# A two-layer trunk on one core: 1/rms from one full product and a power of 256 columns, caches and memory handed in as they are used

## The chip, the cores and the metric

The kernel runs on one core of a Trainium2 chip. Its engines take their instructions in the order in which they are written: TensorE (PE; PEld is its weight load), VectorE (DVE), ScalarE (ACT), GpSimd (POOL), and SyncE (SP), which here only issues transfers; ACT and POOL issue some as well. The metric is the device time of one execution in microseconds, from the start of the program to its end, with inputs and weights in the chip's memory.

## What is computed

Two layers; 128 prompt tokens and 128 sample tokens go through the same weights, so that all products run on 256 columns, one for each token. A layer is a half-step of a gated FFN, a token mixer (differential attention, a 2-D Fourier transform and a bidirectional mLSTM, merged with gates) and a second half-step. Ahead of each of the three stands a norm with modulation:

```python
def rms_norm(x, g):
    y = xf * lax.rsqrt(jnp.mean(xf * xf, axis=-1, keepdims=True) + EPS)
    return (y * g).astype(x.dtype)

u  = modulate(rms_norm(x, g[1]), sh2, sc2)      # x * (1 + scale) + shift
z  = u @ w_in
# sample tokens: keys and values are [cached | own], own keys rotated
k_use = concatenate([k_ctx, apply_rope(k, cos, sin)]); v_use = concatenate([v_ctx, v])
# mLSTM of the sample tokens starts from the cached memory C0, n0, m0
x = x + gt2 * token_mixer(u)
```

The prompt tokens' keys, values and final memories are outputs (`new_cache_k`, `new_cache_v`, `new_state_C` and two small ones), beside the two token blocks.

## The kernel before, in words

**Layout.** The state `xT` is [128, 8, 256]: feature within a block of 128, block k = 0..7, token. A weight comes in chunks of 1 MB (`raw`, by SP), and each chunk is split into a high part `whi` (a cast on ACT, L1523) and a low part `wlo` (a subtraction on DVE, L1524); so is each activation (`hilo`, L177 and L178). Every product with a weight is three matmuls (`mm3`, L165 to L168): high by high, high by low, low by high. Small products and transposes in plain float32 go through `mm` (L163) and `trans` (L171). `pm`, `pa`, `pb` are tiles of PSUM.

**Order.** The order is the order of the code. A list of `steps` (units of the projections) is run from first to last; small work of the attention, Fourier, gate and mLSTM parts is written as generators, "lanes", each `yield` of which ends one lane step. A lane step is run from the middle of a product of eight blocks (`mid`), so that a lane's matmuls stand between those of the projections in TensorE's row. The splits of coming weight chunks are pumped in the same manner.

**A norm.** While the residual is added block by block, `square` squares the block on ACT and POOL adds it into `nsum` [128, 256] (L413; the last square stays apart as `last`), and `block`/`parts` make y = x * (1 + scale), not yet divided by the rms, with its high and low part (`yf` L426, `yh` L177, `yl` L178). The last two blocks are held back (`held`). Then `first` (L523) starts the next projection: four units (512 columns of the weight) on y, for k = 0 to 7. After k = 0 it makes 1/rms: `stats` sums over the features with four matmuls of one column each (`pb` 128x2), `root` makes `var` on DVE (L463) and the power -1/2 on POOL (L465), `diag` puts the two columns of 1/rms on the diagonals of two matrices `dg` (one on DVE, L469, one on ACT), and `spread`, after k = 1, multiplies a matrix of ones with them, so that all partitions hold the row of 256 values, which ACT copies from PSUM to `bcs`. Then `apply` makes u = y * bcs + shift in two halves of four blocks: L486 (times), L491 (plus), `uh` on ACT (L492), `ul` on DVE (L495). The four units on y are corrected with `bcs` as they leave PSUM (`scaled`, L552). All further products of the projection read u. `first` is called five times: for the two mixers and for three FFNs; the first norm of the program and the last one are made in another way.

**Caches and memory.** In a mixer, `loads` and `loads2` issue the transfers of the narrow gate weights `zgw` (on POOL) and of the cached keys and values `ckv` and the memory `C0` (on ACT), each rearranged by the transfer's access pattern. The attention lane transposes the four heads' cached keys (L171 into `pa`) and copies them into the first half of `kl`, has the rotary swap of q brought into the other half of `kl` by four transfers (L822), rotates, does the same for k, transposes the prompt's k for the output `new_cache_k` (copy `kctx` on ACT, transfer on POOL), and comes to scores, softmax and values (transposed probabilities `pc`). The gate lane transposes the eight blocks of `C0` into `c0t`.

Of the kernel before, what the change touches and what calls it, by code (L numbers as in the profile page):

```python
# [14 lines left out]
ALU = mybir.AluOpType  # L15
AX = mybir.AxisListType

P = 128
D = 1024
# [3 lines left out]
H = 4  # L23
# [99 lines left out]
def trunk_kernel(ctx: ExitStack, tc: tile.TileContext, a: dict):  # L123
# [12 lines left out]
    def blk(shape, name, dt=F32):  # L136
        return blkp.tile(shape, dt, tag="blk", name=name)
# [4 lines left out]
    def t2(shape, name, dt=F32):  # L142
        return tp.tile(shape, dt, tag="t2", name=name, bufs=N_T2)
# [240 lines left out]
    class Norm:  # L384
# [81 lines left out]

        def diag(self):
            dg = self.dg = t2([P, 2, P], "dg")
            ve.tensor_scalar(dg[:, 0, :], ident, self.rstd[:, 0:1], None, op0=ALU.mult)  # L469
            ac.activation(dg[:, 1, :], ident, AF.Copy, scale=self.rstd[:, 1:2])  # L470

        def spread(self):
            bc = pb([P, 256])
            mm(bc, ones, flat(self.dg))
            self.bc = tmp([P, 256], "bcs", bufs=1)
            ac.copy(self.bc, bc)

        def apply(self):
# [44 lines left out]
    def first(norm, us, done, func=None):  # L523

        ps = first_tiles()
        for k in range(KD):
            first_k(norm.yk, k, us, ps)
            if k == 0:
                norm.stats()
                warm(func)  # L530
                held.pop(0)()
                norm.diag()
                while held:
                    held.pop(0)()
                pump_split(1)
            if k == 1:
                norm.spread()
        norm.apply()
        pump_split(1)

        def rest():
            done(norm, ps)
            pump_split()

        late.append(rest)
# [146 lines left out]
    def add_mixer(l, norm, norm_next, mods_):  # L692
# [3 lines left out]
        def loads():  # L696
            M["zgw"] = tmp([P, KD, 16], "zgw", bufs=1)
            po.dma_start(out=M["zgw"], in_=w_in[:, 4096:4112].rearrange("(k p) f -> p k f", p=P))

        def loads2():  # L700
            ac.preload_act_table_set("natural_log_exp_and_others")
            M["ck"] = blk([P, 2, H, P], "ckv")
            nc.scalar.dma_start(out=M["ck"][:, 0], in_=a["cache_k"][0, l].rearrange("h s d -> s h d"))
            nc.scalar.dma_start(out=M["ck"][:, 1], in_=a["cache_v"][0, l].rearrange("h s d -> s h d"))
            M["C0"] = blk([P, 2, H, P], "C0")
            nc.scalar.dma_start(out=M["C0"], in_=a["state_C"][0, l].rearrange("d h v k -> v d h k"))
            gh, gl = M["gh"], M["gl"] = blk([P, KD, 104], "zgh", F32R), blk([P, KD, 104], "zgl", F32R)
# [95 lines left out]
        def attn_lane():  # L803
            q = M["q"]
            ql = q[:, :, T:]
            kl = blk([P, H, 256], "kl")
            yield
            yield
            t = pa([P, H, P])
            for h in range(H):  # L810
                trans(t[:, h, :], M["ck"][:, 0, h, :])
            yield
            ve.tensor_copy(kl[:, :, 0:128], t)
            cosb = cst[:, C_COS:C_COS + 128].unsqueeze(1).to_broadcast([P, H, T])
# [21 lines left out]
            yield  # L836
            t = pa([P, H, P])
            for h in range(H):
                trans(t[:, h, :], k[:, h, 0:T])
            yield  # L840
            kn = t2([P, H, P], "kctx")
            ac.copy(kn, t)
            po.dma_start(out=a["new_cache_k"][0, l].rearrange("h s d -> s h d"), in_=kn)
            yield
# [115 lines left out]
            for h in range(H):  # L960
                for c in range(2):
                    vv = M["ck"][:, 1, h, :] if c == 0 else M["v"][:, 1, h * P:(h + 1) * P]
                    mm(o[:, h, :], pTl[h // 2][:, 2 * (h % 2) + c, :], vv, start=(c == 0), stop=(c == 1))
# [42 lines left out]
        def gate_lane():  # L1006
# [69 lines left out]
            for g in range(2):  # L1076
                M["w"][g] = blk([P, 2, H, T], f"w{g}")
                for d in range(2):
# [5 lines left out]
                    for h in range(H):  # L1084
                        ac.activation(M["w"][g][:, d, h, :], E[:, h, :], AF.Exp,
                                      bias=gT[:, g, 32 * d + h:32 * d + h + 1])
            yield
            c0t = M["c0t"] = blk([P, H, 2, 129], "c0t")
            ve.tensor_copy(c0t[:, :, :, 128],
                           parT[1][:, 96 + 8 * l:104 + 8 * l].rearrange("p (d h) -> p h d", d=2))  # L1090
            for d in range(2):
                t = pb([P, H, P])
                for h in range(H):
                    trans(t[:, h, :], M["C0"][:, d, h, :])
                yield
                ve.tensor_copy(c0t[:, :, d, 0:128], t)

# [438 lines left out]
    for s in steps:  # L1536
# [16 lines left out]
        for fn in late:  # L1553
# [4 lines left out]

_INS = ["x_prompt", "x_sample", "cache_k", "cache_v", "state_C", "attn_lambda", "w_ada", "w_ffn1_in",
        "w_ffn1_out", "w_ffn2_in", "w_ffn2_out", "w_in", "w_branch_gate", "w_br_attn", "w_br_four",  # L1560
        "w_br_mlstm", "w_out"]
_OUTS = [("y_prompt", (1, T, D)), ("y_sample", (1, T, D)),
         ("new_cache_k", (1, DEPTH, H, T, 128)), ("new_cache_v", (1, DEPTH, H, T, 128)),
         ("new_state_C", (1, DEPTH, 2, H, 128, 128)), ("new_state_n", (1, DEPTH, 2, H, 128)),
# [3 lines left out]
def _arrays(inputs):  # L1568
# [6 lines left out]
    wt = inputs["w_ada"].reshape(DEPTH, D, N_MOD, KD // 2, 2, P)  # L1575
    arrays["w_adaT"] = np.ascontiguousarray(wt.transpose(0, 2, 3, 5, 4, 1))
    return arrays

# [16 lines left out]
```

## Time and profile before

| | us |
|---|---|
| median of three runs | 1338.78 (1338.4 to 1339.75) |
| the profiled execution | 1340.14 |
| its span, first to last instruction | 1338.4 |
| TensorE busy | 1306.4 (98%) |
| VectorE busy | 1038.2 (78%) |
| ScalarE busy | 659.8 (49%) |
| POOL busy | 68.0 (5%) |
| mean granted clock of TensorE | 0.990 of full speed |

The rows below come from that one profiled execution. In a timeline a row gives the start and the duration in us, the engine, the line, the operation, what it writes and reads, and in brackets how long the engine stood idle before it and who ended that. Lines are those of the kernel before.

### The profile page before, as it was taken

The numbers are of one execution on the slowest core, as the hardware profiler recorded it, in microseconds if no ns is written. First come the engines' busy times: TensorE is split into PE (matmuls) and PEld (weight loads), VectorE is DVE, ScalarE is ACT, GpSimd is POOL, SyncE is SP. The second block draws the span as 40 slices with busy tenths as digits, with TensorE's granted clock in tenths as the row PEclk, the third lists the DMA queues.
The fourth block names the chain that finished last, engine by engine and source line by source line (L and its number), as shares of the span: only waits on it lengthen the run. The fifth ranks groups of instructions, "written<-read, shape, count | busy, mean of one in ns | idle before, by whom it ended". The sixth has DMA issues, their size and how long they took to land. (4 is left out here: it accounts for less than half of the span.)

```text
span 1338.4 us, 25512 instructions
## 1 busy us (share of the span) xinstructions
PE 1306.4 (98%) x10584; PEld 1256.4 (94%) x10584; DVE 1038.2 (78%) x1652; ACT 659.8 (49%) x1026; POOL 68.0 (5%) x88
## 2 busy tenths in 40 slices
PE   8999999899999998999999999989999999999998
PEld 6999999788999997999999999988999899999998
DVE  5798897687678888888979988876677889895553
ACT  4654444565554454444445544455555446554442
POOL 0000001000000020000000000110000001000001
PEclk9999999899999999999999999999999999999999
DMA  9999774745567538887748977856446766495520
GB/s 377 373 336 357 242 260 163 239 139 189 190 227 260 191 130 302 277 297 264 249 155 280 302 256 252 279 167 191 158 135 200 273 228 208 164 310 188 168 96 32
DMA packets 221587, 304.70 MB, mean 228 GB/s; under 512 B 5584, under 2 KB 194272, under 8 KB 214176
## 3 DMA queue, kind: packets, MB, share of 16 engines
q1 hardware_dynamic: 213760, 295.93, 65.8%
q10 hardware_dynamic: 6640, 4.20, 1.2%
q0 software_dynamic: 1072, 2.95, 0.6%
q8 instruction: 83, 1.36, 0.4%
q14 instruction: 32, 0.26, 0.1%
HBM read 298.85 MB, written 3.15 MB: 226 GB/s over the span
## 5 line engine op out<-in xcount | busy, mean ns | idle before, releaser
L1524 DVE TENSOR_TENSOR wlo<-raw,whi 128x1024 fp32r<-128x1024 f32 (+1 forms) x428 | 507.3, 1192 | 219.3 <-ACT whi L1523 217.1
L1523 ACT CAST whi<-raw 128x1024 fp32r<-128x1024 f32 (+1 forms) x428 | 434.6, 1024 | 298.7 <-PE pm L167 211.9
L166 PE MATMUL pm<-uh,whi 128*128 128x256 f32 x1904 | 546.9, 287 | 0.0
L167 PE MATMUL pm<-ul,whi 128*128 128x256 f32 x1904 | 538.3, 283 | 1.0 <-DVE ul L495 0.9
L168 PE MATMUL pm<-uh,wlo 128*128 128x256 f32 x1904 | 538.2, 283 | 0.4 <-DVE wlo L1524 0.3
L166 PEld LDWEIGHTS pm<-uh,whi 128*128 128x128 f32 x1904 | 363.0, 191 | 12.6 <-issue 7.1
L167 PEld LDWEIGHTS pm<-ul,whi 128*128 128x128 f32 x1904 | 362.7, 190 | 2.5 <-DVE ul L495 2.1
L168 PEld LDWEIGHTS pm<-uh,wlo 128*128 128x128 f32 x1904 | 362.4, 190 | 0.9 <-DVE wlo L1524 0.8
L319 DVE CUSTOM_DVE_ANT_0 junkw<-raw,cb 128x1024 bf16<-128x1024 f32 x192 | 233.7, 1217 | 0.0
L168 PE MATMUL pm<-hh,wlo 128*128 128x256 f32 x640 | 179.6, 281 | 0.0
L166 PE MATMUL pm<-hh,whi 128*128 128x256 f32 x640 | 179.5, 280 | 0.0
L167 PE MATMUL pm<-hl,whi 128*128 128x256 f32 x640 | 179.5, 280 | 0.0
L168 PEld LDWEIGHTS pm<-hh,wlo 128*128 128x128 f32 x640 | 120.7, 189 | 0.0
L166 PEld LDWEIGHTS pm<-hh,whi 128*128 128x128 f32 x640 | 120.6, 188 | 0.0
L167 PEld LDWEIGHTS pm<-hl,whi 128*128 128x128 f32 x640 | 120.5, 188 | 0.0
L413 POOL TENSOR_TENSOR nsum<-nsum,nsq 128x256 f32<-128x256 f32 x36 | 36.1, 1002 | 816.7 <-issue 436.7
L657 ACT ACTIVATE silu<-pm 128x512 f32<-128x512 f32 x38 | 22.7, 596 | 54.9 <-PE pm L168 54.9
L411 ACT ACTIVATE nsq<-xT 128x256 f32<-128x256 f32 x42 | 17.5, 417 | 53.2 <-DVE xT L570 53.1
L177 ACT CAST hh<-silu 128x512 fp32r<-128x512 f32 x37 | 22.8, 620 | 41.4 <-DVE silu L659 41.4
L570 DVE SCALAR_TENSOR_TENSOR xT<-pm,mod,xT 128x128 f32<-128x128 f32 x96 | 28.7, 342 | 17.4 <-PE pm L168 17.3
L760 PE MATMUL pm<-whi,uh 128*128 128x512 f32 x96 | 39.3, 410 | 0.0
L761 PE MATMUL pm<-wlo,uh 128*128 128x512 f32 x96 | 37.9, 395 | 0.0
(339 smaller groups left out, 1751.4 us busy)
## 6 DMA issues: line engine op xcount, KB each, us to landing
raw<-w_ffn_in SPq DMA_DIRECT2D x82, 1024.0 KB, 6.8
raw<-w_adaT SPq DMA_DIRECT2D x48, 1024.0 KB, 5.0
raw<-w_ffn_out SPq DMA_DIRECT2D x32, 1024.0 KB, 5.0
raw<-w_in SPq DMA_DIRECT2D x32, 1024.0 KB, 5.8
raw<-w_ada SPq DMA_DIRECT2D x24, 1024.0 KB, 6.9
raw<-w_branch_gate SPq DMA_DIRECT2D x24, 1024.0 KB, 5.2
raw<-w_ffn_out SPq DMA_DIRECT2D x16, 768.0 KB, 6.0
raw<-w_out SPq DMA_DIRECT2D x8, 1024.0 KB, 5.0
```

Source lines behind the costliest of these rows:

```text
L166: pe.matmul(out, sh, mh, start=start, stop=False)
L167: pe.matmul(out, sh, ml, start=False, stop=False)
L168: pe.matmul(out, sl, mh, start=False, stop=stop)
L177: ac.copy(hi, src)
L319: ve.tensor_tensor_reduce(junkw, u.raw()[:, 0, :], cb[:, g, :], 1.0, 0.0, op0=ALU.mult, op1=ALU.add, accum_out=o[:, k, g:g + 1])
L413: eng.tensor_add(self.sum, self.sum, sq)
L570: ve.scalar_tensor_tensor(xT[:, k, G[g]], ps[:, G[g]], gate[:, k, g:g + 1], xT[:, k, G[g]], op0=ALU.mult, op1=ALU.add)
L657: ac.activation(st["s"], st["a"], AF.Silu)
L760: pe.matmul(ps[g], xh[:, G[g]], wh, start=(k == 0), stop=False)
L761: pe.matmul(ps[g], xh[:, G[g]], wl, start=False, stop=False)
L1523: ac.copy(u.hi, r)
L1524: ve.tensor_sub(u.lo, r, u.hi.bitcast(F32))
```

## The change

1. `first` calls a new function `rows` after k = 0. Two matmuls with the full 128x128 matrix of ones give the sum of squares of all 256 tokens on every partition at once (`pb` 128x256); DVE makes mean + eps from it into `bcs`, and POOL raises the 128x256 to the power -1/2 in place. The one-column products, the power of two columns, the diagonals, the second product and the copy out of PSUM are gone there. Both held blocks follow right behind `rows`.
2. The host hands in the cached keys and values, the memory and the narrow gate weights in the order in which the tiles hold them; keys go straight into `kl`, the memory into `c0t`. Their transposes and copies are gone. `new_cache_k` is written as k lies, with no transposes, by a transfer on ACT, and turned on the host.
3. The lanes have fewer steps by what was removed, so what stands behind in them comes earlier in the row of TensorE.

```diff
@@ class Norm @@
+        def rows(self):
+            ss = pb([P, 256])
+            mm(ss, ones, self.sum, start=True, stop=False)
+            mm(ss, ones, self.last, start=False, stop=True)
+            self.bc = tmp([P, 256], "bcs", bufs=1)
+            ve.tensor_scalar(self.bc, ss, 1.0 / D, EPS, op0=ALU.mult, op1=ALU.add)
+            po.tensor_tensor(self.bc, self.bc, expo[:, 0:1].to_broadcast([P, 256]), op=ALU.pow)
@@ def first @@
             if k == 0:
-                norm.stats()
+                norm.rows()
                 warm(func)
-                held.pop(0)()
-                norm.diag()
                 while held:
                     held.pop(0)()
                 pump_split(1)
-            if k == 1:
-                norm.spread()
         norm.apply()
@@ def loads, loads2 @@
-            po.dma_start(out=M["zgw"], in_=w_in[:, 4096:4112].rearrange("(k p) f -> p k f", p=P))
+            nc.scalar.dma_start(out=M["zgw"], in_=a["w_inz"][l])
...
-            nc.scalar.dma_start(out=M["ck"][:, 0], in_=a["cache_k"][0, l].rearrange("h s d -> s h d"))
-            nc.scalar.dma_start(out=M["ck"][:, 1], in_=a["cache_v"][0, l].rearrange("h s d -> s h d"))
-            M["C0"] = blk([P, 2, H, P], "C0")
-            nc.scalar.dma_start(out=M["C0"], in_=a["state_C"][0, l].rearrange("d h v k -> v d h k"))
+            M["cv"] = blk([P, H, P], "cv")
+            nc.scalar.dma_start(out=M["cv"], in_=a["cache_vT"][l])
+            M["c0t"] = blk([P, H, 2, 129], "c0t")
+            nc.scalar.dma_start(out=M["c0t"][:, :, :, 0:128], in_=a["state_CT"][l])
@@ def attn_lane @@
             kl = blk([P, H, 256], "kl")
-            yield
-            yield
-            t = pa([P, H, P])
-            for h in range(H):
-                trans(t[:, h, :], M["ck"][:, 0, h, :])
-            yield
-            ve.tensor_copy(kl[:, :, 0:128], t)
+            nc.scalar.dma_start(out=kl[:, :, 0:128], in_=a["cache_kT"][l])
+            yield
+            yield
...
-            t = pa([P, H, P])
-            for h in range(H):
-                trans(t[:, h, :], k[:, h, 0:T])
-            yield
-            kn = t2([P, H, P], "kctx")
-            ac.copy(kn, t)
-            po.dma_start(out=a["new_cache_k"][0, l].rearrange("h s d -> s h d"), in_=kn)
+            nc.scalar.dma_start(out=a["new_cache_k"][0, l], in_=k[:, :, 0:T])
@@ gate lane @@
-            c0t = M["c0t"] = blk([P, H, 2, 129], "c0t")
+            c0t = M["c0t"]
...
-            for d in range(2):
-                t = pb([P, H, P])
-                for h in range(H):
-                    trans(t[:, h, :], M["C0"][:, d, h, :])
-                yield
-                ve.tensor_copy(c0t[:, :, d, 0:128], t)
```

TensorE's row in the `first` of the first mixer, behind the first block k = 0 (`pa` is the fourth unit's tile, `pm` the first unit's at k = 1; `nsq` is the last square):

```order
 L168 MATMUL pa<-yh_2094,wlo 128x258
-L163 MATMUL pb<-ones,nsum 128x1
-L163 MATMUL pb<-ones,nsq 128x1
-L163 MATMUL pb<-ones,nsum 128x1
-L163 MATMUL pb<-ones,nsq 128x1
+L163 MATMUL pb<-nsum,ones 128x256
+L163 MATMUL pb<-nsq,ones 128x256
 L166 MATMUL pm<-yh_2094,whi 128x258
```

Four products of one column, with the sums as the fixed operand, became two of 256 columns, with the ones as the fixed operand.

VectorE's row at the same place, before, from the statistics to the first product of `apply` (`yf_2099` and `yl_2097` hold the last four blocks, `mod_4_100` is 1 + scale):

```order
L463 TENSOR_SCALAR var<-pb 128x2
L426 TENSOR_SCALAR yf_2099<-xT,mod_4_100 128x128
L178 TENSOR_TENSOR yl_2097<-yf_2099,yh_2095 128x256
L469 TENSOR_SCALAR dg<-cst,rstd 128x128
L426 TENSOR_SCALAR yf_2099<-xT,mod_4_100 128x128
L178 TENSOR_TENSOR yl_2097<-yf_2099,yh_2095 128x256 x2
L1524 TENSOR_TENSOR wlo<-raw_2390,whi 128x1024
L486 TENSOR_TENSOR yf_2098<-yf_2098,bcs 128x1024
```

and after:

```order
L485 TENSOR_SCALAR bcs<-pb 128x256
L426 TENSOR_SCALAR yf_2099<-xT,mod_4_100 128x128
L178 TENSOR_TENSOR yl_2097<-yf_2099,yh_2095 128x256
L426 TENSOR_SCALAR yf_2099<-xT,mod_4_100 128x128
L178 TENSOR_TENSOR yl_2097<-yf_2099,yh_2095 128x256 x2
L1513 TENSOR_TENSOR wlo<-raw_2390,whi 128x1024
L496 TENSOR_TENSOR yf_2098<-yf_2098,bcs 128x1024
```

The mean of 256 columns stands where `var` stood, the diagonal is gone from between the two held blocks, and the rest keeps its order (L496 is the L486 of before, L1513 the L1524).

ScalarE's row at the start of the first mixer's lanes, before (transfers are rows here too; `k<-pm` is the key projection's copy out of PSUM):

```order
L701 ACT_TABLE_LOAD
L703 DMA ckv<-cache_k 128x4x128
L704 DMA ckv<-cache_v 128x4x128
L706 DMA C_2882<-state_C 128x8x128
L1523 CAST whi<-raw_2518 128x1024
L740 COPY k<-pm 128x512
L1523 CAST whi<-raw_2518 128x1024
L1523 CAST whi<-raw_2580 128x1024
L822 DMA kl<-q 32x4x128 x4
L740 COPY k<-pm 128x512
```

and after:

```order
L707 ACT_TABLE_LOAD
L709 DMA cv<-cache_vT 128x512
L711 DMA c0t<-state_CT 128x8x128
L812 DMA kl<-cache_kT 128x4x128
L1512 CAST whi<-raw_2518 128x1024
L745 COPY k<-pm 128x512
L1512 CAST whi<-raw_2518 128x1024
L823 DMA kl<-q 32x4x128 x4
L1512 CAST whi<-raw_2580 128x1024
L745 COPY k<-pm 128x512
```

The keys' transfer stands behind the memory's now and goes to `kl`, and the four transfers of the swap are issued one cast earlier.

## Rows read from the trace of the kernel before

**Rows 1.** The page: busy us, share of the span and instructions of each engine.
```profile
PE 1306.4 (98%) x10584; PEld 1256.4 (94%) x10584; DVE 1038.2 (78%) x1652; ACT 659.8 (49%) x1026; POOL 68.0 (5%) x88
```

**Rows 2.** TensorE's waits: instruction <- what ended the wait: us, times, longest.
```profile
PE pa L171 <- DMA ckv<-cache_k: 9.6, 2, 4.9
PE pa L171 <- DVE pc L873: 3.3, 2, 1.6
PE pm L167 <- DVE ul L495: 0.9, 3, 0.4
```

**Rows 3.** Timeline of TensorE: the transposes of the cached keys, first mixer.
```profile
243.65 1.09 PE L171 MATMUL pa<-cst,ckv 128*128 128x128 f32 x4 [4.93 <-DMA ckv<-cache_k]
```

**Rows 4.** Windows: us, busy of PE, PEld, DVE, ACT, POOL, clock, DMA share, GB/s.
```profile
240.00:244.00 4.00, 0.35 (x2) 0.38 (x3) 3.58 (x10) 3.97 (x6) 0.00 (x0) 0.74 1.08 330
244.00:248.00 4.00, 4.00 (x21) 4.00 (x20) 2.37 (x3) 1.75 (x2) 0.00 (x0) 0.50 1.13 330
248.00:252.00 4.00, 4.00 (x27) 3.77 (x27) 1.83 (x2) 1.30 (x3) 0.00 (x0) 0.90 1.02 297
```

**Rows 5.** Timeline of VectorE, first mixer: from `var` to the first product of `apply`.
```profile
219.34 0.16 DVE L463 TENSOR_SCALAR var<-pb 128x2 f32<-128x2 f32 x1 [1.60 <-PE pb L163]
...
220.33 1.52 DVE L469 TENSOR_SCALAR dg<-cst,rstd 128x128 f32<-128x128 f32 x1 [0.28 <-POOL rstd L465]
...
224.54 1.22 DVE L486 TENSOR_TENSOR yf<-yf,bcs 128x1024 f32<-128x1024 f32 x1
```

**Rows 6.** Timeline of POOL, the same place: the power.
```profile
219.58 0.72 POOL L465 TENSOR_TENSOR rstd<-var,expo 128x2 f32<-128x2 f32 x1 [2.63 <-DVE var L463]
```

**Rows 7.** Timeline of VectorE, an FFN's `first`: the same chain.
```profile
686.70 0.16 DVE L463 TENSOR_SCALAR var<-pb 128x2 f32<-128x2 f32 x1 [1.65 <-PE pb L163]
...
688.14 0.28 DVE L426 TENSOR_SCALAR yf<-xT,mod 128x128 f32<-128x128 f32 x1
...
691.10 1.22 DVE L486 TENSOR_TENSOR yf<-yf,bcs 128x1024 f32<-128x1024 f32 x1
```

**Rows 8.** By tile `bcs`, VectorE out of PSUM: ns shortest/median/longest, first and last start.
```profile
L552 DVE TENSOR_TENSOR ft<-pm,bcs x10: 413/416/416, 236.2 to 1157.6; 128x256 f32<-128x256 f32 x10
```

**Rows 9.** By line, POOL's powers and its add: the same columns.
```profile
L465 POOL TENSOR_TENSOR rstd<-var,expo x7: 707/716/746, 10.4 to 1331.0; 128x2 f32<-128x2 f32 x7
L1190 POOL TENSOR_TENSOR mss<-mss,expo x4: 1007/1007/1010, 395.5 to 1078.2; 128x4 f32<-128x4 f32 x4
L899 POOL TENSOR_TENSOR ov<-ov,expo x4: 1037/1226/1415, 300.6 to 1029.8; 128x4 f32<-128x4 f32 x4
L413 POOL TENSOR_TENSOR nsum<-nsum,nsq x36: 725/877/2202, 173.8 to 1327.9; 128x256 f32<-128x256 f32 x36
```

**Rows 10.** Timelines of VectorE and POOL: `yf` beside an add, `yl` beside a power.
```profile
473.52 1.25 POOL L413 TENSOR_TENSOR nsum<-nsum,nsq 128x256 f32<-128x256 f32 x1 [2.81 <-ACT nsq L411]
474.08 0.77 DVE L426 TENSOR_SCALAR yf<-xT,mod 128x128 f32<-128x128 f32 x1
...
486.42 0.71 POOL L465 TENSOR_TENSOR rstd<-var,expo 128x2 f32<-128x2 f32 x1 [1.38 <-DVE var L463]
486.78 0.43 DVE L178 TENSOR_TENSOR yl<-yf,yh 128x256 fp32r<-128x256 f32 x1 [0.24 <-ACT yh L177]
```

**Rows 11.** Timeline of TensorE: the spread, and transposes of `k` with the next product.
```profile
222.00 0.67 PE L163 MATMUL pb<-dg,ones 128*128 128x256 f32 x2 [1.16 <-DVE yf L426]
...
257.71 0.60 PE L171 MATMUL pa<-cst,k 128*128 128x128 f32 x4
258.06 0.48 PE L760 MATMUL pm<-whi,uh 128*128 128x512 f32 x1
258.38 0.39 PE L761 MATMUL pm<-wlo,uh 128*128 128x512 f32 x1
```

**Rows 12.** Transfers `kl<-q`: KB each, median us from issue to landing; VectorE's wait for them.
```profile
kl<-q ACTq DMA_DIRECT2D x8, 64.0 KB, 6.2
...
  DMA kl<-q: 0.4, 1
```

More of the change, by code (lines that the diff above doesn't have):

```diff
@@ L697, in loads @@
             M["zgw"] = tmp([P, KD, 16], "zgw", bufs=1)
-            po.dma_start(out=M["zgw"], in_=w_in[:, 4096:4112].rearrange("(k p) f -> p k f", p=P))
+            nc.scalar.dma_start(out=M["zgw"], in_=a["w_inz"][l])
         def loads2():
             ac.preload_act_table_set("natural_log_exp_and_others")
-            M["ck"] = blk([P, 2, H, P], "ckv")
-            nc.scalar.dma_start(out=M["ck"][:, 0], in_=a["cache_k"][0, l].rearrange("h s d -> s h d"))
-            nc.scalar.dma_start(out=M["ck"][:, 1], in_=a["cache_v"][0, l].rearrange("h s d -> s h d"))
-            M["C0"] = blk([P, 2, H, P], "C0")
-            nc.scalar.dma_start(out=M["C0"], in_=a["state_C"][0, l].rearrange("d h v k -> v d h k"))
+            M["cv"] = blk([P, H, P], "cv")
+            nc.scalar.dma_start(out=M["cv"], in_=a["cache_vT"][l])
+            M["c0t"] = blk([P, H, 2, 129], "c0t")
+            nc.scalar.dma_start(out=M["c0t"][:, :, :, 0:128], in_=a["state_CT"][l])
             gh, gl = M["gh"], M["gl"] = blk([P, KD, 104], "zgh", F32R), blk([P, KD, 104], "zgl", F32R)
@@ L961, in attn_lane @@
                 for c in range(2):
-                    vv = M["ck"][:, 1, h, :] if c == 0 else M["v"][:, 1, h * P:(h + 1) * P]
+                    vv = M["cv"][:, h, :] if c == 0 else M["v"][:, 1, h * P:(h + 1) * P]
                     mm(o[:, h, :], pTl[h // 2][:, 2 * (h % 2) + c, :], vv, start=(c == 0), stop=(c == 1))
@@ L1556, in trunk_kernel @@
     assert not any(lanes)
-_INS = ["x_prompt", "x_sample", "cache_k", "cache_v", "state_C", "attn_lambda", "w_ada", "w_ffn1_in",
+_INS = ["x_prompt", "x_sample", "attn_lambda", "w_ada", "w_ffn1_in",
         "w_ffn1_out", "w_ffn2_in", "w_ffn2_out", "w_in", "w_branch_gate", "w_br_attn", "w_br_four",
@@ L1562 @@
 _OUTS = [("y_prompt", (1, T, D)), ("y_sample", (1, T, D)),
-         ("new_cache_k", (1, DEPTH, H, T, 128)), ("new_cache_v", (1, DEPTH, H, T, 128)),
+         ("new_cache_k", (1, DEPTH, 128, H, T)), ("new_cache_v", (1, DEPTH, H, T, 128)),
          ("new_state_C", (1, DEPTH, 2, H, 128, 128)), ("new_state_n", (1, DEPTH, 2, H, 128)),
@@ L1576, in _arrays @@
     arrays["w_adaT"] = np.ascontiguousarray(wt.transpose(0, 2, 3, 5, 4, 1))
+    wz = inputs["w_in"][:, :, 4096:4112].reshape(DEPTH, KD, P, 16)
+    arrays["w_inz"] = np.ascontiguousarray(wz.transpose(0, 2, 1, 3))
+    arrays["cache_kT"] = np.ascontiguousarray(inputs["cache_k"][0].transpose(0, 3, 1, 2))
+    arrays["cache_vT"] = np.ascontiguousarray(inputs["cache_v"][0].transpose(0, 2, 1, 3))
+    arrays["state_CT"] = np.ascontiguousarray(inputs["state_C"][0].transpose(0, 4, 2, 1, 3))
     return arrays
@@ L1593 @@
     r = run_bass_kernel_spmd(nc, [arrays], core_ids=[0])
-    return tuple(r.results[0][n] for n, _ in _OUTS)
+    out = {n: r.results[0][n] for n, _ in _OUTS}
+    out["new_cache_k"] = out["new_cache_k"].transpose(0, 1, 3, 4, 2)
+    return tuple(out[n] for n, _ in _OUTS)
```

## The prediction

> **What bounds the kernel now.** I read the busy times first: TensorE works 98% of the span [rows 1], so the time is its work plus the few places where it waits. The next view is therefore TensorE's idle time by what ended it [rows 2]. Two kinds of it matter here. The largest single item, 9.6 us in two waits, is the transfer of the cached keys: the transposes that open the attention lane stand in TensorE's row and wait for it. And each `first` ends in a wait on VectorE's `ul`, or ends level with it: there TensorE runs out of products on the un-normalised y and needs u, which needs 1/rms. The five `first` places have almost no slack, so whatever is added between the sum of squares and `apply` moves the end by as much.
>
> The wait for the keys costs twice. TensorE stood 4.93 us until 243.65 [rows 3]; the stretches from there read a granted clock of 0.50 and 0.90 where 1.00 is 2.4 GHz [rows 4]: 0.35 us at half, 4 at 0.50 and 4 at 0.90, that is 0.18 + 2.0 + 0.4 = 2.6 us of lost work.
>
> **What the change does to 1/rms.** Take the chain on VectorE from `var` to the first product of `apply` (L486). In a mixer it is 219.34 to 224.54 = 5.20 us, with the diagonal and the spread in it [rows 5]; in an FFN it is 686.70 to 691.10 = 4.40 us [rows 7]. Two `first` are mixers, three are FFNs. After the change the same stretch holds:
> - the mean over 256 columns read from PSUM in place of `var`: 0.41 us, by the rows of the same engine on the same shape out of PSUM [rows 8];
> - 0.08 us from VectorE to POOL (`var` ends at 219.50, POOL starts at 219.58) [rows 5, 6];
> - the power itself on 128x256 in place of 128x2;
> - the tail from the power to L486.
>
> The power is the term on which all hangs, and no row shows it on 256 columns. Two widths are shown: 128x2 takes 716 ns (seven times, 707 to 746), 128x4 takes 1007 ns (four times, 1007 to 1010) [rows 9]. That is 291 ns for two columns, 145.5 for one; the straight line gives 0.716 + 254 x 0.1455 = 37.67 us. The bound above: the other 128x4 power (L899) spans 1.037 to 1.415 us, median 1.226 [rows 9]; the line through its shortest one, (1037 - 716)/2 = 160 ns a column, gives 41.5 us, the one through its median 65. The bound below: POOL adds 128x256 in 0.725 us at best [rows 9], under 3 ns a column, and a power on 256 columns can't be cheaper than an add. I take the straight line, since it is through rows of the same operation on the same engine with almost no spread, and 256 columns are 128 times two columns.
>
> The Trainium skill ("GPSIMD Engine Reference", § 3.1 "Elementwise — side-by-side cycle accounting") puts an elementwise instruction with two inputs at about 2.6 cycles for an element of a partition, the engine's clock at 1.2 GHz. By that, an estimate, 256 columns are 0.55 us and a dispatch, which the add's 0.725 bears out; the two rows of the power, 145 ns a column, are some 65 times off it, and it has no price for a power. The first rival below is what would happen at such a rate.
>
> The tail. One VectorE instruction of `block`, `yf` (L426), is still to come after the mean, and then the parts, one `wlo` and `apply`. If `yf` runs beside the power, all of that is long done when the power ends, and L486 starts at once (0.03 us). If it stands until POOL lets go, the tail is what ran from `yf` to L486 in the FFN: 688.14 to 691.10 = 2.96 us [rows 7]. For the second: the same `yf` that takes 0.28 took 0.77 beside a POOL add and ended with it, 474.85 against 474.77 [rows 10]. Against: `yl` ran 0.43 from 486.78 through the end of a power that lasted to 487.13 [rows 10]. The row with `yf` itself is the nearer one; I take 2.96.
>
> The Trainium skill ("SBUF — State Buffer", "Who interferes with whom") says that GpSimd shares one pair of ports with VectorE, and that whoever has it holds it for a whole instruction, against VectorE's instructions in a two-port mode and, where GpSimd reads SBUF, those with two inputs in SBUF. The `yf` row agrees, the `yl` row does not; with it the sum is 1516 us, without it 1501.
>
> So the stretch is 0.41 + 0.08 + 37.67 + 2.96 = 41.1 us: +35.9 in each mixer, +36.7 in each FFN, 71.8 + 110.1 = **+182 us**. With the short tail it is 38.2: 2 x 33.0 + 3 x 33.8 = +167. Nothing hides it: TensorE's row has no other work between the end of the raw products and the first that needs u, and it reaches that point within some tenths of a microsecond of `ul` today [rows 2].
>
> After idle spans this long the clock is lost as after the 4.93 us: 5 x 2.6 = **+13 us** (0 if the fall has another cause).
>
> What TensorE saves at these places, four one-column products, the diagonal's product and a wait of 1.16 us for `yf` ahead of it [rows 11], was ahead of a wait on `ul` and is worth nothing. `new_cache_k` moves from POOL's queue to ScalarE's, `zgw` likewise; nobody waits for either within the mixer.
>
> **What the layouts do.** The keys now land straight in `kl` and are first read by the scores, many microseconds on, so the two waits go: **-9.6 us**. With them go the half-clock stretches behind them: 2 x 2.6 = **-5.2** (0 to -5.2). Sixteen transposes per layer go (four of the cached keys, four of k, eight of the memory): four take from 257.71 to 258.06 and hold up the next product by 0.09 more, 0.44 for a group; eight groups are **-3.5 us** [rows 11]. What is late next there is the rotary swap: its four transfers come 6.2 us after their issue, and VectorE waited 0.4 us for them [rows 12]; the lane is now shorter ahead of it, so up to 3 us a layer may come back, 0 to +6. I take 0, since the swap's readers are on VectorE, not on TensorE. Together -18.3 us.
>
> **Sum.** 182 + 13 - 18.3 = +176.7 on the profiled execution's 1340.14 us, or 1516.8; the median of the runs is 1.36 lower: **1516 us**.
>
> **Rivals.**
> First, faster: the power is cheap. The 291 ns between two and four columns would be a step and not a rate, and the 256 columns would run as POOL's add does, 0.73 to 1.0 us. For it: one engine does 128x256 adds in the time of a 128x2 power. Against: the two tight rows. The stretch is then 0.49 + 0.73 + 2.96 = 4.18 us: 2 x 1.0 + 3 x 0.2 = -2.7 us, and -18.3: 1319, by the median **1318**; with +6 from the swap 1324. This rival is the other side of my forecast. Its point of decision: with the long tail five stretches of (t + 3.45) against 2 x 5.20 + 3 x 4.40 = 23.6, and 18.3 gained, give t = 4.9 us; with the short tail 7.9. So the change is faster if a column costs less than 19 to 31 ns.
>
> Second, in between: the long instruction works in a loop that the short ones don't reach, at a third of the line's rate, 12 us. Then 5 x 15.45 - 23.6 = +53.6, +13 for the clock, -18.3: **1387**. No row speaks for it but the distance between the add and the power.
>
> Third, the layouts gain nothing, because TensorE waits for the swap or for `kl` in place of the keys: 1516 + 18 = 1534 with the straight line. The rows of the swap speak against it [rows 12]. It changes no sign.
>
> **How the numbers follow.** Straight line 0.50 (1495 to 1535 by tail, clock and the 160 ns slope: 0.36, of which 0.05 with the third rival; above, towards L899's median: 0.14); in between 0.10; cheap power 0.36; break-even, t between 4.9 and 7.9, 0.04. A measurement of this kernel tells a change of about 0.2% from none, so: faster 0.36, same 0.04, slower 0.60. The range 1312 to 1535 leaves out the 0.14 above and little below (1312 is the cheap power with the two waits on `pc`, 3.3 us [rows 2], and some half clock behind them gone too, as the lane is shorter ahead of them); the likeliest case's own range is 1495 to 1535.
>
> **What would show it.** POOL's row of `bcs` on 128x256: near 38 us, or near 1. TensorE's waits on `ul`: five of some 33 us, or some tenths. `yf` L426 beside the power: 0.28 us, or ending with it. The transposes' wait for the keys gone, and the granted clock at 1.00 through the first 20 us of that stretch; at 0.5 after each power if that is long. The forecast is wrong if the power's time is no line in its columns, since every other term is small beside it.

## The result

| | before | after |
|---|---|---|
| median, us | 1338.8 (1338.4 to 1339.75) | 1516.28 (1514.92 to 1519.47) |
| span of the profiled run, us | 1338.4 | 1516.8 |
| TensorE busy, us | 1306.4 | 1311.9 |
| POOL busy, us | 68.0 | 266.2 |
| mean granted clock | 0.990 | 0.93 |

The ratio is 1.1328 (95% interval 1.1308 to 1.1348): 177.5 us slower, where 1516 had been forecast. The page of after, busy time by engine, the three rows of the 40 slices that tell most (tenths of a slice; the clock in tenths of full speed), and the costliest row of POOL by form:

```profile
PE 1311.9 (86%) x10521; PEld 1259.5 (83%) x10522; DVE 1033.9 (68%) x1641; ACT 655.7 (43%) x1014; POOL 266.2 (18%) x84
...
PE   8999990999999909999918999928999999099998
POOL 0000029000000470000190000190000004800000
PEclk9999995999999959999968999968999999589999
...
L486 POOL TENSOR_TENSOR bcs<-bcs,expo 128x256 f32<-128x256 f32 x5 | 205.7, 41139 | 12.6 <-DVE bcs L485 9.6 <-DMA raw<-w_in 3.0
```

Five dark places in TensorE's row, five bright ones in POOL's, and the clock at 5 to 6 tenths in the same slices. One power of 256 columns takes 41.14 us, in place of the 0.716 us of two columns [rows 9]. TensorE's waits in after (what waited, for whom: us, times, longest), which answer to [rows 2]:

```profile
PE pm L166 <- ACT uh L502: 176.3, 5, 35.3
PE pm L167 <- DVE ul L505: 6.1, 10, 0.7
PE pa L171 <- DVE pc L868: 5.5, 2, 2.9
PE pd L163 <- DMA raw<-w_ada: 3.7, 2, 2.0
PE pb L171 <- DVE ha L1181: 3.4, 2, 2.0
PE pm L765 <- ACT v L775: 1.5, 1, 1.5
```

The keys' 9.6 us are gone. In their place stand five waits of 35.3 us on the high part of u (ScalarE's `uh` is the last link of the chain, the power its cause), and longer waits on `pc`, `ha` and `v`. Of these three only the one on `ha` is longer beyond doubt: the same kernel run again (e11_again, below) has 3.4 us for `ha` too, but 3.3 for `pc` and none for `v`.

The chain itself, in the first mixer, which answers to [rows 5, 6]: POOL's timeline of after, and then VectorE's (start, duration, line, what; in brackets the idle time ahead and who ended it):

```profile
221.13 41.16 POOL L486 TENSOR_TENSOR bcs<-bcs,expo 128x256 f32<-128x256 f32 x1 [2.98 <-DMA raw<-w_in]
```

```profile
220.63 0.42 DVE L485 TENSOR_SCALAR bcs<-pb 128x256 f32<-128x256 f32 x1 [1.69 <-PE pb L163]
220.97 0.28 DVE L426 TENSOR_SCALAR yf<-xT,mod 128x128 f32<-128x128 f32 x1
221.16 0.86 DVE L178 TENSOR_TENSOR yl<-yf,yh 128x256 fp32r<-128x256 f32 x1
221.95 0.28 DVE L426 TENSOR_SCALAR yf<-xT,mod 128x128 f32<-128x128 f32 x1
222.15 0.41 DVE L178 TENSOR_TENSOR yl<-yf,yh 128x256 fp32r<-128x256 f32 x1
...
262.32 1.23 DVE L496 TENSOR_TENSOR yf<-yf,bcs 128x1024 f32<-128x1024 f32 x1 [37.40 <-POOL bcs L486]
```

From the mean (220.63) to the first product of `apply` (262.32) it is 41.69 us; 41.1 had been forecast. Two of its terms were off, and they cancel. The power took 3.47 us more than the straight line gave. And `yf` wasn't held up: the one at 220.97 began ahead of the power, the one at 221.95 ran 0.28 us beside it. `apply` starts 0.03 us after the power's end (221.13 + 41.16 = 262.29), not 2.96.

### The profile page after: what moved, and what is told of

Read it like the earlier page. It is cut to its first block, busy times and chain, and to the rows that moved or that the text cites. A ratio compares the mean times of both kernels' runs of the same rounds, so it can differ in the third digit from the quotient of the medians.

```text
span 1516.8 us, 25380 instructions
## 1 busy us (share of the span) xinstructions
PE 1311.9 (86%) x10521; PEld 1259.5 (83%) x10522; DVE 1033.9 (68%) x1641; ACT 655.7 (43%) x1014; POOL 266.2 (18%) x84
## 4 chain that ended last, share of the span: by engine, by line
PE 68%; POOL 14%; DVE 10%; ACT 3%; DMA 2%; issue 2%; ACTq 0%; SPq 0%; DVEq 0%; POOLq 0%
PE pm L166 20%; PE pm L167 20%; PE pm L168 20%; POOL bcs L486 14%; DVE wlo L1513 4%; PE pd L163 2%; PE pb L163 2%; ACT whi L1512 1%; DMA kl<-q 1%; DMA raw<-w_ada 1%; DVE junkw L319 1%; DVE yf L496 1%; DVE yf L501 1%; DVE ul L505 1%; PE pa L163 1%
## 5 line engine op out<-in xcount | busy, mean ns | idle before, releaser
L166 PE MATMUL pm<-uh,whi 128*128 128x256 f32 x1904 | 550.8, 289 | 176.3 <-ACT uh L502 176.3
L1513 DVE TENSOR_TENSOR wlo<-raw,whi 128x1024 fp32r<-128x1024 f32 (+1 forms) x428 | 506.9, 1191 | 212.3 <-ACT whi L1512 210.1
L166 PEld LDWEIGHTS pm<-uh,whi 128*128 128x128 f32 x1904 | 366.7, 193 | 188.6 <-ACT uh L502 177.3
L486 POOL TENSOR_TENSOR bcs<-bcs,expo 128x256 f32<-128x256 f32 x5 | 205.7, 41139 | 12.6 <-DVE bcs L485 9.6
L496 DVE TENSOR_TENSOR yf<-yf,bcs 128x1024 f32<-128x1024 f32 x10 | 12.2, 1221 | 186.9 <-POOL bcs L486 186.9
L502 ACT CAST uh<-yf 128x1024 fp32r<-128x1024 f32 x10 | 10.5, 1046 | 217.9 <-DVE yf L501 217.9
```

What stands on the lines that cost most here:

```text
L166: pe.matmul(out, sh, mh, start=start, stop=False)
L486: po.tensor_tensor(self.bc, self.bc, expo[:, 0:1].to_broadcast([P, 256]), op=ALU.pow)
L496: ve.tensor_mul(us[i], us[i], bc)
L1513: ve.tensor_sub(u.lo, r, u.hi.bitcast(F32))
```

## The experiments

Comparisons are with the kernel before on the same chip; its median was 1338.9 to 1339.9 in the five groups of runs.

**The parts, each alone.** The layouts with the old way to 1/rms:

```diff
@@ first, of the changed kernel @@
-                norm.rows()
+                norm.stats()
                 warm(func)
+                held.pop(0)()
+                norm.diag()
...
+            if k == 1:
+                norm.spread()
```

> The change with its layouts alone: keys, values, memory and gate weights as used, no transposes for them; 1/rms made as before (one-column products, power of 2 columns, diagonals, second product). Theory: the layouts gain what the sum said, 9.6 us of waits, 5.2 us of half clock and 3.5 us of transposes, so 1338.8 - 18.3 = 1320.5 (1319 to 1326 with the swap late). Rival (the wait moves to the swap or to the new place of the keys): 1336 to 1339, with a wait of 4 us or more on TensorE in each mixer.

And `rows` in the kernel before, with its layouts as they were (the same piece of `first` the other way round):

> The kernel before with rows() alone, layouts as before. Theory (the terms add up): five stretches longer by 36.5 (mixers) and 37.3 us (FFNs), +184.9, and five times some 2.6 us of half clock behind them, +13: 1338.8 + 198 = 1537 (1530 to 1540). Without a loss by the clock: 1524. Rival (the long power gives the cached keys time to land, so that their waits go here as well and the two parts overlap): 1537 - 9.6 - 5.2 = 1522.

Measured: e1_layouts 1330.77, ratio 0.9934 (0.9911 to 0.9958), 8.8 us faster. Half of what was expected, and clear of the rival too. e2_rows 1526.95, ratio 1.1402 (1.1367 to 1.1438), 187.7 us slower: ten less than the sum of the terms. Two of TensorE's waits in e2_rows:

```profile
PE pa L171 <- DMA ckv<-cache_k: 3.3, 1, 3.3
PE pa L171 <- DVE zgh L718: 2.2, 1, 2.2
```

The rival is there in part: TensorE waits for the keys once, 3.3 us, and 2.2 us on the high part of the gate weights (`zgh`), where the kernel before waits 9.6 us for the keys. The two parts add up: 0.1402 - 0.0066 = 0.1336, and the changed kernel has 0.1328. So an overlap of the parts is too small to show in these intervals (some 6 us together), but the two smaller terms of the sum, clock and layouts, were forecast much larger than they are, with opposite signs. The runs below go after both.

**The power.** First, the changed kernel without it:

```diff
-            ve.tensor_scalar(self.bc, ss, 1.0 / D, EPS, op0=ALU.mult, op1=ALU.add)
-            po.tensor_tensor(self.bc, self.bc, expo[:, 0:1].to_broadcast([P, 256]), op=ALU.pow)
+            ve.tensor_scalar(self.bc, ss, 0.0, -1.0, op0=ALU.mult, op1=ALU.add)
+            po.tensor_tensor(self.bc, self.bc, expo[:, 0:1].to_broadcast([P, 256]), op=ALU.mult)
```

> The changed kernel with a POOL multiplication of 128x256 by -0.5 in place of the power, on a row of -1 (the division by the rms is left out: every token is scaled by 0.5). Theory: the power alone makes the change slow; the stretch is 0.42 + 0.08 + some 0.9 + at most 3.0 = 4.4 us, 0.8 less than before in the mixers and level in the FFNs, and the layouts gain 18.3: 1319 (1317 to 1326). Rival (full products with ones, both held blocks in one go and the new order cost of their own): 1330 or more. Beside the multiplication, yf on VectorE: 0.28 us if POOL doesn't hold it up, some 0.7 if it does as in the row of before.

Measured: 1330.73, ratio 0.9932 (0.991 to 0.9954). The median is that of e1_layouts within 0.04 us: the rest of the new way to 1/rms is worth nothing and costs nothing that these intervals show, and the loss is the power's. (1319 fell with the layouts' 18.3. The rival's 1330 is reached, but e1_layouts, which keeps the old way, has it too.) The stretch from the mean to `apply` is 5.28 us in the mixers and 4.22 in the FFNs here, about as long as before (5.20 and 4.40). Then half of the power:

```diff
-            po.tensor_tensor(self.bc, self.bc, expo[:, 0:1].to_broadcast([P, 256]), op=ALU.pow)
+            po.tensor_tensor(self.bc[:, 0:128], self.bc[:, 0:128], expo[:, 0:1].to_broadcast([P, 128]), op=ALU.pow)
+            po.tensor_tensor(self.bc[:, 128:256], self.bc[:, 0:128], expo[:, 0:1].to_broadcast([P, 128]), op=ALU.mult)
```

> The changed kernel with the power on 128 of the 256 columns; the other 128 are filled by a POOL multiplication from the first (the sample tokens' own 1/rms is left out). Theory (the price goes by columns, 159 ns each): each power 41.1 - 20.4 = 20.8 us, plus some 0.5 for the filling, so 1516.3 - 5 x 19.9 = 1417. Rival (a fixed price of a long instruction, or steps): a power of 35 us or more and 1490, or one far under 20.

Measured: 1416.93 (1413.0 to 1420.8, two runs) where the theory had 1417, the power 20.74 us. Over e1_layouts that is 86 us, where the whole power costs 186: the price goes by columns. Last the price by itself, on POOL where it has nothing else to do:

```diff
@@ s_loads, of the kernel before @@
+        lad = blk([P, 256], "lad")
+        po.memset(lad, 1.7)
+        for n in (1, 2, 4, 8, 16, 32, 64, 128):
+            po.tensor_tensor(lad[:, 0:n], lad[:, 0:n], expo[:, 0:1].to_broadcast([P, n]), op=ALU.pow)
+        for n in (2, 4, 32, 256):
+            po.tensor_tensor(lad[:, 0:n], lad[:, 0:n], expo[:, 0:1].to_broadcast([P, n]), op=ALU.mult)
+        for p in (16, 32, 64):
+            po.tensor_tensor(lad[0:p, 0:32], lad[0:p, 64:96], expo[0:p, 0:1].to_broadcast([p, 32]), op=ALU.pow)
...     # 32 columns of 0.0001 (L271), 32 of 900 (L273), 8 with a whole tile of exponents (L274)
```

> The kernel before with powers and multiplications of several widths on POOL where it stands idle (from 52 us on): powers of 1, 2, 4, 8, 16, 32, 64 and 128 columns on 128 partitions, multiplications of 2, 4, 32 and 256 columns, powers of 32 columns on 16, 32 and 64 partitions, and on values 0.0001 and 900. Theory (each column is a step of its own in which all partitions go together): 0.4 us + 0.159 us a column, 128 columns 20.8 us, the same for 16, 32, 64 and 128 partitions, and for each value. Rival A (groups of columns): equal times within a group and steps between. Rival B (price by elements): 16 partitions take an eighth of 128. Rival C (price by value): 0.0001 and 900 differ from 1.7 by more than 0.3 us at 32 columns. Multiplications of 2 and 4 columns: 0.2 us or less, if the 0.4 us are the power's own. The whole time stays within 1337 to 1342, since POOL has nothing else to do there.

POOL's groups by line and form (form, count, busy us, mean ns); L265 are the powers, L267 the multiplications, L269 the powers on fewer partitions:

```profile
L265 POOL TENSOR_TENSOR lad<-lad,expo 128x128 f32<-128x128 f32 x1 | 21.5, 21523 | 0.1
L265 POOL TENSOR_TENSOR lad<-lad,expo 128x64 f32<-128x64 f32 x1 | 10.6, 10599 | 0.1
L269 POOL TENSOR_TENSOR lad<-lad,expo 16x32 f32<-16x32 f32 x1 | 6.3, 6274 | 0.1
L265 POOL TENSOR_TENSOR lad<-lad,expo 128x32 f32<-128x32 f32 x1 | 5.9, 5908 | 0.1
L269 POOL TENSOR_TENSOR lad<-lad,expo 32x32 f32<-32x32 f32 x1 | 5.5, 5526 | 0.1
L271 POOL TENSOR_TENSOR lad<-lad,expo 128x32 f32<-128x32 f32 x1 | 5.4, 5417 | 0.1
L273 POOL TENSOR_TENSOR lad<-lad,expo 128x32 f32<-128x32 f32 x1 | 5.4, 5416 | 0.1
L269 POOL TENSOR_TENSOR lad<-lad,expo 64x32 f32<-64x32 f32 x1 | 5.4, 5412 | 0.1
L265 POOL TENSOR_TENSOR lad<-lad,expo 128x16 f32<-128x16 f32 x1 | 2.9, 2915 | 0.1
L265 POOL TENSOR_TENSOR lad<-lad,expo 128x8 f32<-128x8 f32 x1 | 1.8, 1763 | 0.1
L265 POOL TENSOR_TENSOR lad<-lad,expo 128x4 f32<-128x4 f32 x1 | 1.7, 1742 | 0.1
L274 POOL TENSOR_TENSOR lad<-lad,expo 128x8 f32<-128x8 f32 x1 | 1.7, 1705 | 0.1
L267 POOL TENSOR_TENSOR lad<-lad,expo 128x32 f32<-128x32 f32 x1 | 1.1, 1097 | 0.1
L267 POOL TENSOR_TENSOR lad<-lad,expo 128x4 f32<-128x4 f32 x1 | 1.1, 1076 | 0.1
L265 POOL TENSOR_TENSOR lad<-lad,expo 128x2 f32<-128x2 f32 x1 | 0.7, 710 | 0.1
L265 POOL TENSOR_TENSOR lad<-lad,expo 128x1 f32<-128x1 f32 x1 | 0.6, 627 | 0.1
L267 POOL TENSOR_TENSOR lad<-lad,expo 128x256 f32<-128x256 f32 x1 | 0.6, 613 | 0.1
L267 POOL TENSOR_TENSOR lad<-lad,expo 128x2 f32<-128x2 f32 x1 | 0.2, 240 | 0.1
```

Some of these rows are too long for their width: the power of 4 columns takes as long as that of 8 (1.007 in [rows 9]), the 32 columns of L265 take 0.49 more than those of L271 and L273, and a multiplication of 4 columns takes more than one of 256. Each of them began while VectorE was in an instruction with two inputs (`wlo`, or `junkw` in the modulation), and is longer by what was left of that instruction, less some 0.14 us. At the power of 4 columns (54.84, VectorE until 55.71) 0.87 us was left, and 0.74 came on top. At the 32 columns it was 0.63 and 0.49, at the 128 (20.74 in e4_half) 0.93 and 0.78, at the 16 partitions 1.01 and 0.86; the two long multiplications end 0.07 and 0.11 us after VectorE. The kernel before has it too, here VectorE's row and POOL's:

```profile
300.43 0.68 DVE L1001 TENSOR_TENSOR fl<-four,fh 128x512 fp32r<-128x512 f32 x1
```

```profile
300.60 1.41 POOL L899 TENSOR_TENSOR ov<-ov,expo 128x4 f32<-128x4 f32 x1 [16.51 <-DVE ov L898]
```

By the rows that met at most 0.22 us of such an instruction the price goes by columns. 8 to 16 is 1.21 us more (151 ns each), 16 to 32 2.50 (156), and 32 to 64 5.18 (162); with the 20.74 of e4_half 64 to 128 is 10.1 (158), and with after's 41.14 128 to 256 is 20.4 (159). Sixteen partitions take no less than 128, and 0.0001 as long as 900. A multiplication of 256 columns takes 0.61 us and one of two 0.24, so the rest is the power's own. All three rivals fall (A and C by these rows alone). The time of this run, 1341.5 beside 1339.9, stayed inside what was expected.

**The layouts: where half of the gain went.** TensorE's waits in e1_layouts:

```profile
PE pd L163 <- DMA raw<-w_ada: 6.7, 3, 2.9
PE pa L171 <- DVE pc L872: 4.7, 2, 2.5
PE pb L171 <- DVE ha L1185: 3.5, 2, 2.0
...
PE pm L769 <- ACT v L779: 1.8, 1, 1.8
```

Against [rows 2] and the other waits of before: keys -9.6; `pc` 3.3 to 4.7, `ha` 1.6 to 3.5, `v` 0 to 1.8, and the weights of the modulation, `w_ada`, 4.7 to 6.7: +7.1 comes back. Not all of that is the layouts' doing: 1.6 of the 2.0 on `w_ada` stand in the first 15 us of the program, ahead of all that they touch, and `pc` and `v` differ by 2.2 and 1.5 us between the two traces of the changed kernel. Stage by stage, from the first product of `apply` to the statistics of the next norm, both mixers are shorter (261.6 to 256.3 and 260.9 to 255.5), and the FFN behind the first one longer (196.1 to 198.0). The lost speed of TensorE (busy time by one less the clock, over the whole span in windows of 4 us) falls from 10.4 to 9.2 us only, since the clock falls behind the new waits as well. So: -9.6 for the keys, -3.5 for the transposes, -1.1 for the clock and +7.1 are -7.1, of the 8.7 by which the two spans differ.

To see the keys' wait alone, only they were moved:

```diff
@@ loads2, of the kernel before @@
-            nc.scalar.dma_start(out=M["ck"][:, 0], in_=a["cache_k"][0, l].rearrange("h s d -> s h d"))
@@ attn_lane @@
             kl = blk([P, H, 256], "kl")
+            nc.scalar.dma_start(out=kl[:, :, 0:128], in_=a["cache_kT"][l])
             yield
             yield
-            t = pa([P, H, P])
-            for h in range(H):
-                trans(t[:, h, :], M["ck"][:, 0, h, :])
             yield
-            ve.tensor_copy(kl[:, :, 0:128], t)
```

> The kernel before with the cached keys alone laid out as used: straight into kl, four transposes and a copy gone in each layer, their lane step left in as an empty one; all else as before. Theory: the keys' wait is worth its 9.6 us and the half clock behind it, 4.8 us by the windows of before, and 0.9 us of transposes: 15 under before, 1324 (or 1327 if the clock falls a second time elsewhere), and pc as before, 3.3 us. Rival (a wait on the swap, on VectorE's copies or on pc takes the place of the keys): 1333 or more.

Measured: 1331.9, ratio 0.9947 (0.9927 to 0.9966): 7 us, with the rival's 6 inside the interval and the theory's 15 far out of it. TensorE's waits, then VectorE's timeline at that place, then ScalarE's (ACT is its own work, ACTq a transfer that it issues):

```profile
PE pd L163 <- DMA raw<-w_ada: 7.3, 4, 3.4
PE pa L163 <- ACT kctx L838: 5.4, 2, 2.7
PE pa L171 <- DVE pc L869: 2.6, 2, 1.5
```

```profile
250.56 0.69 DVE L823 TENSOR_TENSOR kl<-kl,cst 128x512 f32<-128x512 f32 x1 [2.18 <-DMA kl<-q]
251.29 0.69 DVE L824 TENSOR_TENSOR q<-rope,kl 128x512 f32<-128x512 f32 x1
```

```profile
252.05 2.62 ACTq L818 DMA_DIRECT2D kl<-k  x4
254.72 1.04 ACT L1519 CAST whi<-raw 128x1024 fp32r<-128x1024 f32 x1 [8.20 <-issue]
...
257.38 0.59 ACT L838 COPY kctx<-pa 128x512 f32<-128x512 f32 x1
```

There is the next wait, 2.7 us in each mixer, and its chain. TensorE's first scores need a PSUM tile that ScalarE's copy `kctx` has to empty. ScalarE stands 8.20 us ahead of the cast at 254.72: its row holds the issue of k's swap, which writes where the rotation of q still reads, and goes out at 252.05, when that is done (251.29 + 0.69); and that rotation had waited 2.18 us for q's own swap (0.40 in [rows 12]). In the kernel before, the keys' wait covered this: ScalarE stood 6.41 us ahead of the cast at 258.86 there, with the same issue (256.19 to 258.81) just ahead of it, and TensorE, later by the wait for the keys, didn't wait for `kctx`. (That ScalarE stands for that issue is read from these times; in e8_keys the row itself names no releaser.) In e1_layouts `kctx` is gone, but ScalarE stands 6.81 us behind the same issue, and `pc` comes later in the same lane. That the issue is what makes `pc` late isn't shown: right ahead of its exponentials (263.17) ScalarE stood 1.80 us for VectorE's maxima.

Then the lane steps that the layouts had taken out were put back as empty ones (four lines `yield`, two in the attention lane and two in the gate lane):

> e1_layouts with the four lane steps per layer that the layouts had taken out put back as empty ones (two in the attention lane, two in the gate lane). Theory: half of the gain was given back because the lanes run ahead of the engines that feed them: the waits on pc (3.3 to 4.7 us), ha (1.6 to 3.5) and v (0 to 1.8) and the half-clock stretches behind them. With the steps back those waits are as in the kernel before and the time is some 5 to 7 us under e1_layouts, 1324 to 1326. Rival (the waits come from the engines' load and not from the steps): within 1.5 us of e1_layouts, 1329 to 1332.

One more step ahead of the transposes of `ha` alone (`if g == 1: yield`):

> e1_layouts with one more empty lane step ahead of the transposes of ha, for the sample tokens alone. Theory: the wait on ha goes from 3.5 us to 1 or less and with it the half clock behind it, 1.7 us in the first mixer; 3 to 4 us under e1_layouts, 1327. Rival (what stands behind in that lane is late next): no more than 1 us.

And both:

> e1_layouts with the four empty lane steps of e6_steps and the one of e7_ha together. Theory (each step only lets a wait be served behind other products, and the two act at different places): ha at 0.5 us or less, pc and v as in e6_steps, some 1.5 us with the half clock under e6_steps: 1325 to 1327. Rival (the lane's end is late next): 1328 to 1331.

| | us | ratio (95%) | `pc` | `ha` | `v` |
|---|---|---|---|---|---|
| e1_layouts | 1330.77 | 0.9934 (0.9911 to 0.9958) | 4.7 | 3.5 | 1.8 |
| e6_steps | 1327.92 | 0.9919 (0.9899 to 0.994) | 5.7 | 1.5 | 4.3 |
| e7_ha | 1326.75 | 0.9908 (0.9886 to 0.993) | 6.2 | 0.5 | 2.6 |
| e9_steps_ha | 1326.09 | 0.9901 (0.9883 to 0.9918) | 5.7 | none | 2.7 |

A step removes the wait that stands behind it: `ha` goes as expected. `pc` and `v` don't go with the steps; there the theory of e6_steps falls, and its time is between the theory's and the rival's. e7_ha and e9_steps_ha came out as their theories had it. Each of the three is under e1_layouts, with intervals that overlap it; all are faster than the kernel before and than the change, e9_steps_ha by 1.0% and 12.6%. A step directly ahead of the transposes of `pc` wasn't tried.

**The clock.** Behind each power the clock is at half, as forecast. Whether that costs 2.6 us each was tested by keeping TensorE at work through the power:

```diff
@@ first, of the changed kernel @@
+        idle = pb([P, 256])
+        for _ in range(76):
+            mm(idle, ones, cst[:, 0:256])
         norm.apply()
```

> The changed kernel with 76 products of a matrix of ones with 256 constant columns, of no use, behind the last product on y in each first: 0.44 us each, as the two products of ones with the sums show, 33.4 of the 35.3 us in which TensorE waits. They take nothing from the path; what they change is the clock with which TensorE starts on u. Theory A (as the prediction has it, half clock costs 2.6 us behind each power): 13 us less, 1503. Theory B (from the stages of the changed kernel against those of e1_layouts: the FFN stages 2.3 us longer, the mixers no longer): 4 to 7 us less, 1509 to 1512. Theory C (the half clock there lies under waits that exist anyway): 1515 to 1517. If the fill is longer than the wait, the stretch grows and shows it.

> The changed kernel once more, on the chip of e10_fill, to compare the two: 1516, ratio 1.133.

e10_fill 1516.29 (ratio 1.1323, 1.1302 to 1.1344), e11_again 1518.0 (1.1335, 1.1316 to 1.1355). That settled nothing: the 76 products ended 2.4 us ahead of `uh`, and in the four waits on `uh` and `ul` that followed the clock fell again. So ten products more (`range(86)`):

> e10_fill with 86 products in place of 76: those took 32.97 us (762.68 to 795.65), after which TensorE still stood 4.5 us in four waits on uh and ul and the clock fell none the less (0.73 from 796). 86 end at 800.0, where both parts of the first half of u are there; TensorE starts on u 1.3 us later than e10_fill (798.7 with its waits), and then runs on without a wait. Theory A (half clock behind the power costs what the windows show, 2.0 to 4.6 us lost in each of five places, less what the late start costs): the clock stays at 1.00 and the time is 7 to 13 us under e11_again, 1505 to 1511. Theory B (the part at half clock lies mostly under waits on uh and ul): within 3 us of e11_again, 1515 to 1521.

1515.09, ratio 1.13 (1.1275 to 1.1325). Windows behind the third power (us; busy of PE, PEld, DVE, ACT, POOL; clock; DMA share; GB/s), first of e11_again, then of e10_fill, then of e12_fill86:

```profile
796.00:806.00 10.00, 4.99 (x25) 4.40 (x26) 8.69 (x8) 4.88 (x5) 0.14 (x1) 0.57 0.00 0
```

```profile
796.00:806.00 10.00, 5.84 (x28) 5.06 (x29) 8.89 (x8) 4.94 (x5) 0.00 (x0) 0.73 0.10 26
```

```profile
796.00:806.00 10.00, 8.97 (x49) 7.79 (x49) 7.92 (x7) 4.13 (x5) 0.90 (x1) 1.00 0.00 0
```

Now the clock stays at 1.00 (2.4 GHz), and the time is 2.9 us under e11_again by the medians, 4.7 by the ratios, with intervals that just overlap: nearer to theory B than to the 7 of theory A, and for 13 us there is no room. But 86 products are more than the wait holds: TensorE starts on u 5.2 us after the power's end, where the changed kernel starts after 3.65, in all five places. The gain is net of that.

Stage by stage the traces say where it is, and where not (us from each power's end to the first sum of the next norm; `first` is called for a mixer, two FFNs, a mixer and an FFN):

| | mixer | FFN | FFN | mixer | FFN |
|---|---|---|---|---|---|
| after | 255.7 | 193.4 | 185.6 | 253.6 | 185.7 |
| e11_again | 255.7 | 193.8 | 183.7 | 254.3 | 185.9 |
| e12_fill86 | 253.3 | 196.4 | 183.4 | 255.2 | 183.4 |

In the third and the fifth, half clock costs some 2.2 us. The 183.7 of e11_again belongs to it: behind that power the clock came back sooner, and 1.8 us of speed were lost where the other four lost 4.0 to 4.7. The FFN behind the first mixer is longer at full clock: its waits on `w_ada` are 4.9 us in place of the 1.8 of after. The second mixer is longer as well, with 5.3 us of waits on `pc` and `v` in place of 2.9. In the first mixer after lost 1.8 us of speed and e11_again 4.7, and both took 255.7 us.

## Why the prediction was right

The time, 1516.28, is the forecast's to 0.3 us, but only its largest step was right for its own reasons; that the total comes so close is luck. The sign, too, was a choice: by its own odds the forecast had 0.36 for this range and 0.36 for a faster kernel.

- **The straight line through two widths of the power.** Right, and it carried the sign: 37.67 forecast, 41.14 measured. The slope was 145.5 ns a column between 2 and 4, and is (41.14 - 0.716) / 254 = 159 over the whole; the upper line, through L899's shortest row at 160, gave 41.5. The bound of 65 had no price in it: L899's long rows (1.415) met a two-input instruction of VectorE with 0.51 us left and are 0.38 longer.
- **The tail of 2.96 us.** Wrong: 0.03. The step that failed is the choice of the nearest row: the `yf` that ran 0.77 beside an add [rows 10] stood there beside another operation of POOL, and beside a power it runs 0.28. (VectorE's row has two `yf` behind the mean, not one; the first begins ahead of the power.) The Trainium skill ("SBUF — State Buffer", "Who interferes with whom") has one engine hold the shared ports for a whole instruction; for a power of 41 us the trace doesn't agree. What the power does hold up is `yl` (two inputs in SBUF), and only at its start: 0.86 us at 221.16 and 0.41 at 222.15, both beside the same 41 us. The `yl` of [rows 10], put down as the weaker evidence, told it. The trace of before had a stronger one, which began 0.03 us after the power of [rows 6] and ended well ahead of it:

```profile
219.61 0.44 DVE L178 TENSOR_TENSOR yl<-yf,yh 128x256 fp32r<-128x256 f32 x1
```

- **The stretch.** 5.20 and 4.40 became 41.69 and 41.67: 2 x 36.5 + 3 x 37.3 = +184.8, where +182 was forecast. Power and tail cancelled: 5 x 3.47 = +17.4, and 5 x 2.93 = -14.7.
- **Nothing hides it, and what TensorE saves there is worth nothing.** Right: 176.3 us of waits, on `uh` in place of the `ul` that was named, and e3_const no faster than e1_layouts.
- **Half clock behind the power, +13.** Its mechanism is there, its size isn't: with the clock kept at 1.00 the gain is 3 to 5 us (e12_fill86), at the edge of what the runs can tell, and net of the later start on u. The step that failed is to take the lost speed of a stretch as lost time in all five places. In two plain FFNs it is (2.2 us each, near the forecast's 2.6); in the FFN behind the first mixer and in the second mixer longer waits on `w_ada`, `pc` and `v` stand in its place. In the first microseconds behind a power TensorE waits for the halves of u anyway (0.68 and 0.55 us at the third place).
- **Layouts, -18.3.** The keys' waits went, but e1_layouts measures -8.8. Two steps failed. The first is "I take 0, since the swap's readers are on VectorE": it passes over ScalarE, which issues k's swap behind that rotation, and with it stand its casts and its copy `kctx`, for which TensorE waited 5.4 us in e8_keys. In e1_layouts some 5 us came back on `pc`, `ha` and `v`; `ha`'s part is the lane step that is missing ahead of it (e7_ha), the cause of the rest stays open. The second is -5.2 for half clock: the lost speed fell by 1.1 us, since the clock falls behind the new waits as well. The third rival had other waits in place of the keys', and in half of its size that is what came, though not on the swap itself.
- Together the two small terms were forecast at -5.3 and are -7.3 (177.5 - 184.8), so their errors cancel as well.

Of the rivals, the cheap power and the one in between fall with the ladder.

## What to carry to other kernels

A price that no row shows can be had from a line through the two widths that are shown, if both are of that very operation and have little spread; a row of another operation on the same engine (the add at 0.73 us) would have been off by a factor of over 50. Rows that are longer than others of their shape are set aside first: see what the other engine was in when they began. A wait that is removed is worth its length less the wait that it covered: look what the next reader needs, through every engine whose row is in order, those that only issue a transfer included. And a sum that comes out to the microsecond proves none of its terms: here two pairs of errors cancelled, and only runs with one part alone told them apart.

## What the runs showed of the hardware

- POOL's power goes by columns, 151 to 162 ns each from 8 columns up, for any number of partitions from 16 to 128 and for values from 0.0001 to 900; 256 columns took 41.13 to 41.16 us, five times. A multiplication of the same shape takes 0.61. The Trainium skill ("GPSIMD Engine Reference", § 3.1) has some 2.6 cycles at 1.2 GHz for an element, an estimate of 0.55 us for the 256: the multiplication's 0.61 is near it (from 2 to 256 columns it grows by 1.5 ns a column, where those cycles make 2.2), the power takes some 70 times as long for a column.
- A power on POOL leaves VectorE nearly alone. In all five places the instruction with two inputs that met the power's start (`yl`) ended 0.90 us after that start, 0.52 to 0.87 us long in place of 0.41, and those behind it ran at their usual pace through the rest. Beside the multiplication of e3_const, which is over in 0.61 us, `yl` ended after the same 0.90; beside a power of two columns it took 0.44. So the length of POOL's instruction isn't what holds VectorE up.
- The other way round, a power or a multiplication on POOL that began while VectorE was in a two-input instruction of 0.7 to 1.4 us was longer by the rest of it, less some 0.14 us: 0.38 to 0.86 us on top where 0.51 to 1.01 were left, in the ladder and in the kernel before.
- TensorE, filled with products of no use up to the end of a 41 us wait, came out at full clock (1.00 where 0.57 stood without them); where the filling ended 2.4 us early and three shorter waits followed, it read 0.73.
